# The value projection of the stick-breaking branch: 256 columns for four row tiles, or 512 columns for two row tiles with the weights loaded twice

## The chip, the cores and the metric

The kernel runs on one NeuronCore of a Trainium2 chip. The metric is device time in microseconds (us) of one execution of the whole program. The median of three runs of the kernel before is 725.48 us (725.17 to 725.5). Five engines work beside each other, each through its own queue in order: TensorE (PE; its weight loads are listed apart as PEld), VectorE (DVE), ScalarE (ACT), GpSimd (POOL) and SyncE (SP, which issues nearly all transfers here).

## The reference

One decoder layer on 512 tokens of width 1024, in float32:

```python
h = rms_norm(x, g_mix)
qa, ka, va, qb, kb, vb, gates = split(h @ w_in)      # widths 6 x 512, then 2 x 1024
ya = moba_attention(rope(qa), rope(ka), va)          # 8 heads of 64
yb = stick_breaking_attention(qb, kb, vb)            # 8 heads of 64
g = sigmoid(gates + b_gate)
x = x + (g[0] * (ya @ w_branch_a) + g[1] * (yb @ w_branch_b)) @ w_out
x = x + conv_glu(rms_norm(x, g_ffn))                 # w_up, depthwise conv, silu gate, w_down
out = rms_norm(x, g_final)
```

What the change touches is `vb`, the 512 x 512 values of the stick-breaking branch: `vb = h @ w_in[:, 2560:3072]`, needed by `yb`.

## The kernel before

Float32 products are made from split operands: every weight tile is loaded as 128 x 1024 float32 (512 KB), ACT rounds it to `whi` and DVE takes the rest `wlo = raw - whi` (`wload`, lines 56 to 70). `mm3` (lines 72 to 75) then issues three matmuls per product: hi x hi, hi x lo, lo x hi. A pool of five `raw` tiles and a pool of three split pairs (`wsp`) hold the weights, so a new split may begin once the tile three places ahead of it has been used up.

The attention stage is `attend` (line 390 on), called four times: twice for branch a (MoBA), twice for branch b (stick-breaking), each for two pairs of heads. Each call has nine steps: three `score` steps (matmuls into `sc`, then softmax weights, or for branch b `weights_b`: sigmoids on ACT, a triangular select on POOL, scans of `a` into `R` and products on DVE), six `turn` steps (transposes on PE into `tp`, copied to `aT`), and at the end the product with v into a last `tp` (line 429), split into `ya` or `yb` by ACT (line 435) and DVE (line 436). PE alone is ordered by hand; the other engines' orders are laid down by a scheduler when the program is built.

Between the steps PE runs **fillers**: generators that issue the remaining projections a piece at a time. `fill(gap)` takes the next `gap` units from a list, one unit being three matmuls of 512 columns (or six of 256). `GAPS_A`, `GAPS_A2` and `GAPS_B` hold the gap after each step. The list before is: q and k of the last MoBA heads (32 units), `sb_qk(0)` and `sb_qk(1)` (q and k of a stick-breaking head pair, 16 units each), `vproj_b(0)`, `sb_qk(2)`, `sb_qk(3)`, `vproj_b(1)`, then three gates of 16 units.

All fillers write to two PSUM banks (`pmm`, tiles `mm`). `proj` (one weight tile, 24 matmuls) uses one bank; whoever takes a bank again waits until its last content has been read out. For `sb_qk` that reading is a DVE product into `o` (lines 304 and 306), which is split later by `flush`. `vproj_b(g)` makes columns 256 g to 256 g + 255 of `vb` for all four row tiles: two weight tiles (one for each half of the 1024 inputs), two row tiles side by side in one bank, 24 matmuls of 256 columns for each; a full bank is read out by ACT (line 251) and DVE (line 252), half each.

Of the kernel before, what the change touches and what calls it, by code (L numbers as in the profile page):

```python
# [10 lines left out]
F32 = mybir.dt.float32  # L11
F32R = mybir.dt.float32r
BF = mybir.dt.bfloat16
AF = mybir.ActivationFunctionType
OP = mybir.AluOpType
# [3 lines left out]
S = 512  # L19
D = 1024  # L20
KT = D // 128
QT = S // 128
# [4 lines left out]
NWARM = 9 * (448,) + (128,)  # L27
NP = FT // 2
NL = 3
WORDER = ([(n, k) for n in ("qk0", "va") for k in range(4)] + [("vb", g, h) for g in range(2) for h in range(2)]  # L30
          + [("mqk", n, i) for n in range(2) for i in range(2)] + [("sqk", p, n) for p in range(4) for n in range(2)]
          + [("g", i, b) for i in range(KT) for b in range(2)] + [("ab", i) for i in range(KT)]
          + [("out", k) for k in range(KT)] + [("ox", j) for j in range(KT // 2)] + [("up", i, b) for i in range(FT) for b in range(2)]
          + [("down", k) for k in range(FT)] + [("dx", j) for j in range(NP)])
WIDX = {k: i for i, k in enumerate(WORDER)}
NEG = -1e30
# [3 lines left out]
def trunk_layer(ctx: ExitStack, tc: tile.TileContext, x: bass.AP, xT: bass.AP, w: bass.AP, vec: bass.AP,  # L40
                gfin: bass.AP, trig: bass.AP, out: bass.AP):
    nc = tc.nc

    def pool(stack, name, bufs, space=None, side=None):
        kw = {}
        if space is not None:
            kw["space"] = space
        if side is not None:
            kw["side"] = side
        return stack.enter_context(tc.tile_pool(name=name, bufs=bufs, reuse_waits="tile", **kw))  # L50
# [5 lines left out]
    def wload(key, pieces=1, eng=None):  # L56
        raw = wraw.tile([128, 1024], F32, name="raw")
        hi = wsp.tile([128, 1024], F32R, name="whi")
        lo = wsp.tile([128, 1024], F32R, name="wlo")
        n = 1024 // pieces  # L60
        for i in range(pieces):
            sl = slice(i * n, (i + 1) * n)
            (eng if eng is not None and i == 0 else nc.sync).dma_start(raw[:, sl], w[WIDX[key]][:, sl])
            if eng is not None and i == 0:
                nc.scalar.preload_act_table_set("sqrt_and_others")
        for i in range(pieces):
            sl = slice(i * n, (i + 1) * n)
            nc.scalar.activation(hi[:, sl], raw[:, sl], AF.Copy)  # L68
            nc.vector.tensor_sub(lo[:, sl], raw[:, sl], hi[:, sl].bitcast(F32))  # L69
        return hi, lo  # L70

    def mm3(ps, a, b, start, stop, **kw):
        nc.tensor.matmul(ps, a[0], b[0], start=start, stop=False, **kw)  # L73
        nc.tensor.matmul(ps, a[0], b[1], start=False, stop=False, **kw)  # L74
        nc.tensor.matmul(ps, a[1], b[0], start=False, stop=stop, **kw)  # L75

    def blk(t, k, n=128):
        return t[0][:, k * n:(k + 1) * n], t[1][:, k * n:(k + 1) * n]
# [23 lines left out]
    xg = [hp.tile([128, 2, S], F32R, name=f"xg{k}") for k in range(KT)]  # L102
# [3 lines left out]
    vb = vp.tile([128, QT, 512], F32, name="vb")  # L106

    def rstd_cols(sq, psp, tag, name):
        ps = psp.tile([128, 512], F32, name=tag)
        for t in range(QT):  # L110
            nc.tensor.matmul(ps[:, 2 * t:2 * t + 2], sq[:, t * 128:(t + 1) * 128], ones, start=True, stop=True)
        v = consts.tile([128, QT], F32, name=name + "v")
        nc.vector.tensor_scalar(v, ps[:, 0:2 * QT:2], 1.0 / D, EPS, op0=OP.mult, op1=OP.add)
        return rsqrt(v, QT, name)
# [19 lines left out]
    pmm = pool(psA, "pmm", 2, PSUM)  # L134
# [7 lines left out]
    qk0 = [p1.tile([128, S], F32, name=f"q{j}") for j in range(4)]  # L142
# [18 lines left out]
    for k in range(KT):  # L161
# [7 lines left out]
        else:  # L169
            if k % 2 == 0:  # L170
# [3 lines left out]
                                             op0=OP.mult, op1=OP.subtract)  # L174
# [9 lines left out]
        for n, (i, j) in enumerate(((0, 0), (0, 1), (1, 0))):  # L184
            if k == KT - 1 and n == 2:
                r1 = rstd_cols(ssq, pmm, "mm", "n1")
# [34 lines left out]
    va = mp.tile([128, QT, 512], F32, name="va")  # L221
# [13 lines left out]
        use(ps)  # L235
        yield 1.0

    def vproj_b(g):
        wt = tuple(wload(("vb", g, h)) for h in range(2))
        for t in range(QT):  # L240
            if t % 2 == 0:
                ps = pmm.tile([128, S], F32, name="mm")
            o = ps[:, (t % 2) * 256:(t % 2 + 1) * 256]
            for k in range(KT):
                a = (xg[k][:, 0, t * 128:(t + 1) * 128], xg[k][:, 1, t * 128:(t + 1) * 128])
                mm3(o, a, blk(wt[k // 4], k % 4, 256), k == 0, k == KT - 1)
                if k < KT - 1:
                    yield 0.5
            if t % 2:
                dst = vb[:, t - 1:t + 1, g * 256:(g + 1) * 256]  # L250
                nc.scalar.activation(dst[:, 0], ps[:, :256], AF.Copy, scale=r1[:, t - 1:t])
                nc.vector.tensor_scalar(dst[:, 1], o, r1[:, t:t + 1], None, op0=OP.mult)
            yield 0.5

    def fill(n):
        while n > 0 and fillers:
# [35 lines left out]
    def moba_qk(g):  # L292
        for n in range(2):
            half = {}
            for i in range(2):
                yield from proj(("mqk", n, i), lambda ps: rotate(g, n, i, ps, half))

    def sb_qk(p):
        sc = {}

        def use(n, nm, ps):
            o = hlp.tile([128, S], F32, name="o")
            if nm == "q":
                nc.vector.scalar_tensor_tensor(o, ps, 0.125, rb, op0=OP.mult, op1=OP.mult)
            else:
                nc.vector.tensor_mul(o, ps, rb)
            sc[nm] = mqkp.tile([128, 2, S], F32R, name=f"hl{n}")
            late.append((sc[nm], o))

        for n, nm in enumerate(("q", "k")):  # L310
            yield from proj(("sqk", p, n), lambda ps: use(n, nm, ps))
        stk["b", p] = [(sc["q"], sc["k"], h * 64) for h in range(2)]
# [145 lines left out]
            yield from proj(("g", i, b), lambda ps: use(b, ps))  # L458

    pend = {}  # L460
    fillers = [moba_qk(1), sb_qk(0), sb_qk(1), vproj_b(0), sb_qk(2), sb_qk(3), vproj_b(1)]
    fillers += [gates(i) for i in range(NG)]
    GAPS_A = (12, 0, 5, 5, 0, 5, 7, 5, 5)
    GAPS_A2 = (10, 0, 3, 6, 0, 3, 6, 3, 3)
    GAPS_B = (8, 4, 5, 4, 3, 5, 7, 5, 5)
    attend("a", (0, 1), GAPS_A)
    attend("a", (2, 3), GAPS_A2, True)
    mst.close()
# [1 line left out]
    for p in range(4):  # L470
        yhl["b", p] = ybp.tile([128, 2, S], F32R, name=f"yb{p}")
    gsig = pool(ysta, "gsig", 6, side="right")
    attend("b", (0, 1), GAPS_B)
    attend("b", (2, 3), GAPS_B)
    fill(1000)
    psA.close()
# [3 lines left out]
    pmm = pool(psB, "pmm2", 6, PSUM)  # L480
# [24 lines left out]
    for i in range(KT):  # L505
# [4 lines left out]
        g = pend[i]  # L510
        for b, br in enumerate("ab"):
            ps = pmm.tile([128, S], F32, name="mm")
# [206 lines left out]
    for i in range(FT):  # L719
        uc = []  # L720
        for b in range(2):
            ps = ups.pop(0) if ups else [*up_mm()][-1]
# [3 lines left out]
            t = up.tile([128, S], F32, name=f"t{b}")  # L726
            nc.scalar.activation(t, u, AF.Identity, bias=cb[:, c:c + 1], scale=cw[:, 2, c:c + 1])  # L727
            nc.vector.scalar_tensor_tensor(t[:, 1:], u[:, :S - 1], cw[:, 1, c:c + 1], t[:, 1:],
                                           op0=OP.mult, op1=OP.add)
            nc.vector.scalar_tensor_tensor(t[:, 2:], u[:, :S - 2], cw[:, 0, c:c + 1], t[:, 2:],  # L730
                                           op0=OP.mult, op1=OP.add)
# [12 lines left out]
    dst = ExitStack()  # L744
# [42 lines left out]
    for j in range(NP):  # L787
        xs, wa, w4, _ = ready.pop(0)
# [66 lines left out]
def pack(w_in, w_a, w_b, w_out, w_up, w_down):  # L855
    def rows(m, c):
        return m[:, c].reshape(m.shape[0] // 128, 128, len(c)).transpose(1, 0, 2).reshape(128, -1)

    c128 = np.arange(128)
    t = {}  # L860

    def halves(base, g, i):
        return base + (4 * g + c128 // 32) * 64 + 32 * i + c128 % 32

    first = np.concatenate([halves(base, 0, i) for base in (0, 512) for i in range(2)])
    for k in range(4):
        t["qk0", k] = rows(w_in[k * 256:(k + 1) * 256], first)
    for n, base in enumerate((0, 512)):
        for i in range(2):
            t["mqk", n, i] = rows(w_in, halves(base, 1, i))  # L870
    for j in range(4):
        t["va", j] = rows(w_in[j * 256:(j + 1) * 256], 1024 + np.arange(512))
    for g in range(2):
        for h in range(2):
            t["vb", g, h] = rows(w_in[h * 512:(h + 1) * 512], 2560 + g * 256 + np.arange(256))
    for p in range(4):
        for n, base in enumerate((1536, 2048)):
            t["sqk", p, n] = rows(w_in, base + p * 128 + c128)
    for i in range(KT):
        for b in range(2):  # L880
            t["g", i, b] = rows(w_in, 3072 + b * 1024 + i * 128 + c128)
        t["ab", i] = np.concatenate([rows(w_a, i * 128 + c128), rows(w_b, i * 128 + c128)], axis=1)
        t["out", i] = w_out[i * 128:(i + 1) * 128]
    for j in range(KT // 2):
        t["ox", j] = np.concatenate([w_out[(2 * j + b) * 128:(2 * j + b + 1) * 128, 512:] for b in range(2)], axis=1)
    for i in range(FT):
        for b in range(2):
            t["up", i, b] = rows(w_up, b * FF + i * 128 + c128)
        t["down", i] = w_down[i * 128:(i + 1) * 128]
    for j in range(NP):  # L890
        t["dx", j] = np.concatenate([w_down[(2 * j + b) * 128:(2 * j + b + 1) * 128, 512:] for b in range(2)], axis=1)
    return np.ascontiguousarray(np.stack([t[k] for k in WORDER]))

# [27 lines left out]
```

## Time and profile before

| | us |
|---|---|
| median of three runs | 725.48 |
| the profiled execution | 725.86 |
| its span, first to last instruction | 724.0 |
| PE busy in the span | 714.3 |
| DVE busy | 554.1 |
| ACT busy | 346.6 |

The profiled execution lies 0.38 us above the median; the trace begins at 0 us with its first instruction. A timeline row gives the start, the busy time, the engine, the line, the operation, its output and inputs, shapes and count, and in brackets the idle time before it and what ended that. Consecutive instructions of one line and operation are merged into one row with a count, even where their shapes differ. A matmul's duration is longer than the distance to the next one's start, since matmuls are pipelined; what a matmul costs is that distance.

### The profile page before, as it was taken

How to read it: one execution, taken by the hardware profiler on the slowest of the kernel's cores; microseconds unless marked ns; L12 is line 12 of the kernel's file. 1: busy time of each engine (PE TensorE's matmuls, PEld its weight loads, DVE VectorE, ACT ScalarE, POOL GpSimd, SP SyncE). 2: the span in 40 equal slices, each digit the busy share in tenths (PEclk: the TensorE clock that was granted, in tenths of full speed). 3: DMA queues.
4: the chain of work that ended last, by engine and by line, in shares of the span. 5: the costliest groups of instructions: out<-in, count | busy, mean ns of one | idle time of the engine just before them, and what ended most of it. 6: DMA issues, size and time to landing. Idle time of an engine off the chain costs nothing.

```text
span 724.0 us, 9741 instructions
## 1 busy us (share of the span) xinstructions
PE 714.3 (99%) x3792; PEld 593.1 (82%) x3792; DVE 554.1 (77%) x795; ACT 346.6 (48%) x506; POOL 22.7 (3%) x40
## 2 busy tenths in 40 slices
PE   9999999999999999999999999999999999999995
PEld 6888888889888888888888888888888888788884
DVE  7778867593973654669878787787787789878996
ACT  6435535463663232337484434443434444556665
POOL 0000000230410000000000000000000000000000
PEclk9999999999999999999999999999999999999998
DMA  8522111021132223225744223223223223467703
GB/s 306 193 88 88 60 59 59 31 88 59 60 96 74 94 87 107 82 103 191 279 148 139 87 88 116 87 88 115 89 88 112 92 88 113 139 213 238 262 24 118
DMA packets 25679, 84.11 MB, mean 116 GB/s; under 512 B 2848, under 2 KB 3488, under 8 KB 25632
## 3 DMA queue, kind: packets, MB, share of 16 engines
q1 hardware_dynamic: 24912, 82.30, 33.8%
q10 hardware_dynamic: 720, 1.18, 0.4%
q8 instruction: 30, 0.49, 0.3%
q14 instruction: 17, 0.14, 0.1%
HBM read 79.27 MB, written 4.19 MB: 115 GB/s over the span
## 4 chain that ended last, share of the span: by engine, by line
PE 95%; DVE 3%; ACT 1%; issue 1%; ACTq 0%
PE b L74 13%; PE b L75 13%; PE b L73 12%; PE mm L73 11%; PE mm L75 11%; PE mm L74 11%; PE c L74 4%; PE c L75 4%; PE c L73 4%; PE q L188 3%; PE tp L429 2%; PE tp L407 2%; PE sc L330 1%; PE sc L340 1%; PE mm L145 1%
## 5 line engine op out<-in xcount | busy, mean ns | idle before, releaser
L68 ACT ACTIVATE whi<-raw 128x1024 fp32r<-128x1024 f32 (+2 forms) x98 | 98.2, 1008 | 166.7 <-PE b L74 80.7
L74 PE MATMUL b<-h,whi 128*128 128x512 f32 x352 | 137.1, 389 | 0.3 <-DVE h L634 0.3
L73 PE MATMUL b<-h,whi 128*128 128x512 f32 x352 | 137.1, 390 | 0.0
L75 PE MATMUL b<-h,wlo 128*128 128x512 f32 x352 | 137.0, 389 | 0.0
L69 DVE TENSOR_TENSOR wlo<-raw,whi 128x1024 fp32r<-128x1024 f32 (+2 forms) x98 | 112.9, 1157 | 14.6 <-ACT whi L68 14.3
L73 PE MATMUL mm<-xg,whi 128*128 128x512 f32 x224 | 90.0, 402 | 0.0
L75 PE MATMUL mm<-xg,wlo 128*128 128x512 f32 x224 | 87.5, 390 | 0.0
L74 PE MATMUL mm<-xg,whi 128*128 128x512 f32 x224 | 87.3, 390 | 0.0
L74 PEld LDWEIGHTS b<-h,whi 128*128 128x128 f32 x352 | 66.1, 188 | 14.3 <-DVE h L634 0.7
L73 PEld LDWEIGHTS b<-h,whi 128*128 128x128 f32 x352 | 66.1, 188 | 13.8
L75 PEld LDWEIGHTS b<-h,wlo 128*128 128x128 f32 x352 | 66.1, 188 | 13.6
L556 ACT ACTIVATE whi<-raw 128x1024 fp32r<-128x1024 f32 x45 | 46.7, 1051 | 33.3 <-DVE raw L568 20.2
L556 DVE TENSOR_TENSOR wlo<-raw,whi 128x1024 fp32r<-128x1024 f32 x45 | 54.3, 1219 | 4.4 <-ACT whi L556 4.4
L725 DVE TENSOR_TENSOR u<-b,rb 128x512 f32<-128x512 f32 x44 | 30.3, 690 | 30.4 <-PE b L75 30.3
L73 PEld LDWEIGHTS mm<-xg,whi 128*128 128x128 f32 x224 | 42.1, 188 | 10.1 <-issue 1.8
L75 PEld LDWEIGHTS mm<-xg,wlo 128*128 128x128 f32 x224 | 42.0, 188 | 9.1
L74 PEld LDWEIGHTS mm<-xg,whi 128*128 128x128 f32 x224 | 42.2, 188 | 7.9
L727 ACT ACTIVATE t<-u,vecs 128x512 f32<-128x512 f32 x44 | 35.2, 802 | 2.1 <-DVE u L725 2.1
L74 PE MATMUL c<-wlo,xa 128*128 128x512 f32 x88 | 34.4, 391 | 0.4 <-DVE wlo L556 0.4
L73 PE MATMUL c<-whi,xa 128*128 128x512 f32 x88 | 34.3, 389 | 0.0
L75 PE MATMUL c<-whi,xa 128*128 128x512 f32 x88 | 34.2, 389 | 0.0
L730 DVE SCALAR_TENSOR_TENSOR t<-u,vecs,t 128x510 f32<-128x510 f32 x44 | 32.9, 749 | 1.3
(219 smaller groups left out, 1260.3 us busy)
## 6 DMA issues: line engine op xcount, KB each, us to landing
raw<-w SPq DMA_DIRECT2D x133, 512.0 KB, 3.3
xk<-xT SPq DMA_DIRECT2D x8, 256.5 KB, 5.6
x<-x SPq DMA_DIRECT2D x4, 512.0 KB, 6.8
x1D<-x SPq DMA_DIRECT2D x8, 256.0 KB, 3.2
x1R<-x1D SPq DMA_DIRECT2D x4, 512.0 KB, 8.1
raw<-w SPq DMA_DIRECT2D x6, 256.0 KB, 5.8
out<-on SPq DMA_DIRECT2D x4, 256.0 KB, 2.2
out<-on ACTq DMA_DIRECT2D x4, 256.0 KB, 2.4
```

What stands on the lines that cost most here:

```text
L68: nc.scalar.activation(hi[:, sl], raw[:, sl], AF.Copy)
L69: nc.vector.tensor_sub(lo[:, sl], raw[:, sl], hi[:, sl].bitcast(F32))
L73: nc.tensor.matmul(ps, a[0], b[0], start=start, stop=False, **kw)
L74: nc.tensor.matmul(ps, a[0], b[1], start=False, stop=False, **kw)
L75: nc.tensor.matmul(ps, a[1], b[0], start=False, stop=stop, **kw)
L188: nc.tensor.matmul(qk0[c], w0[i][:, (k % 2) * 512 + c * 128:(k % 2) * 512 + (c + 1) * 128], xg[k][:, j], start=(k == 0 and n == 0), stop=( ...
L407: nc.tensor.transpose(tp[:, h, c:c + 128], a[:, h, c:c + 128], ident)
L429: nc.tensor.matmul(av[h * 64:(h + 1) * 64, j, qt * 128:(qt + 1) * 128], v[:, kb, (2 * p + h) * 64:(2 * p + h + 1) * 64], aT[p][:, h, o + k ...
L556: splits.append((nc.scalar.activation(hi, raw, AF.Copy), nc.vector.tensor_sub(lo, raw, hi.bitcast(F32))))
L725: nc.vector.tensor_mul(u, ps, rb2)
L727: nc.scalar.activation(t, u, AF.Identity, bias=cb[:, c:c + 1], scale=cw[:, 2, c:c + 1])
L730: nc.vector.scalar_tensor_tensor(t[:, 2:], u[:, :S - 2], cw[:, 0, c:c + 1], t[:, 2:], op0=OP.mult, op1=OP.add)
```

## The change

`vproj_b(T)` now makes all 512 columns of `vb` for row tiles 2T and 2T + 1. It holds both banks, one for each row tile, and goes through four weight tiles of 256 inputs x 512 columns each, which are laid out as those of `va` are. `vproj_b(0)` and `vproj_b(1)` each load all four, so eight weight tiles are loaded and split where there were four. The first row tile's bank is read out by ACT, the second's by DVE, 512 columns in one instruction. In the list of fillers both calls stand ahead of `sb_qk(2)` and `sb_qk(3)`. The first branch-b call of `attend` takes its gaps from a new tuple `GAPS_B1` with 52 units in place of 46. The number of units over all fillers is unchanged, 176; the four calls' gaps sum to 170 before and 176 after.

```diff
-WORDER = ([(n, k) for n in ("qk0", "va") for k in range(4)] + [("vb", g, h) for g in range(2) for h in range(2)]
+WORDER = ([(n, k) for n in ("qk0", "va", "vb") for k in range(4)]
...
-    def vproj_b(g):
-        wt = tuple(wload(("vb", g, h)) for h in range(2))
-        for t in range(QT):
-            if t % 2 == 0:
-                ps = pmm.tile([128, S], F32, name="mm")
-            o = ps[:, (t % 2) * 256:(t % 2 + 1) * 256]
-            for k in range(KT):
-                a = (xg[k][:, 0, t * 128:(t + 1) * 128], xg[k][:, 1, t * 128:(t + 1) * 128])
-                mm3(o, a, blk(wt[k // 4], k % 4, 256), k == 0, k == KT - 1)
-                if k < KT - 1:
-                    yield 0.5
-            if t % 2:
-                dst = vb[:, t - 1:t + 1, g * 256:(g + 1) * 256]
-                nc.scalar.activation(dst[:, 0], ps[:, :256], AF.Copy, scale=r1[:, t - 1:t])
-                nc.vector.tensor_scalar(dst[:, 1], o, r1[:, t:t + 1], None, op0=OP.mult)
-            yield 0.5
+    def vproj_b(T):
+        ps = [pmm.tile([128, S], F32, name="mm") for _ in range(2)]
+        for j in range(4):
+            wt = wload(("vb", j))
+            for i in range(2):
+                t = 2 * T + i
+                for k in range(2 * j, 2 * j + 2):
+                    a = (xg[k][:, 0, t * 128:(t + 1) * 128], xg[k][:, 1, t * 128:(t + 1) * 128])
+                    mm3(ps[i], a, blk(wt, k % 2, 512), k == 0, k == KT - 1)
+                    if k < KT - 1:
+                        yield 1.0
+                if j == 3:
+                    if i:
+                        nc.vector.tensor_scalar(vb[:, t], ps[i], r1[:, t:t + 1], None, op0=OP.mult)
+                    else:
+                        nc.scalar.activation(vb[:, t], ps[i], AF.Copy, scale=r1[:, t:t + 1])
+                    yield 1.0
...
-    fillers = [moba_qk(1), sb_qk(0), sb_qk(1), vproj_b(0), sb_qk(2), sb_qk(3), vproj_b(1)]
+    fillers = [moba_qk(1), sb_qk(0), sb_qk(1), vproj_b(0), vproj_b(1), sb_qk(2), sb_qk(3)]
...
+    GAPS_B1 = (8, 4, 6, 5, 3, 6, 8, 6, 6)
...
-    attend("b", (0, 1), GAPS_B)
+    attend("b", (0, 1), GAPS_B1)
```

The first place is PE at the start of `vproj_b(0)`, around the transposes of one `turn` step, the last six of which fall here (`tp`; `mm` is the bank, numbers tell buffers apart). Before:

```order
L73 MATMUL mm_1333<-whi_1322,xg3_95 128x256
L74 MATMUL mm_1333<-wlo_1323,xg3_95 128x256
L75 MATMUL mm_1333<-whi_1322,xg3_95 128x256
L407 MATMUL tp_1346<-ident_67,a1_1197 128x128 [waits DVE_49,Activation_49]
L407 MATMUL tp_1346<-ident_67,a1_1197 128x128 x2
L407 MATMUL tp_1346<-ident_67,a1_1197 128x128 [waits DVE_49]
L407 MATMUL tp_1346<-ident_67,a1_1197 128x128 x2
L73 MATMUL mm_1333<-whi_1328,xg4_96 128x256
```

Now:

```order
L73 MATMUL mm_1321<-whi_1324,xg1_93 128x512
L74 MATMUL mm_1321<-wlo_1325,xg1_93 128x512
L75 MATMUL mm_1321<-whi_1324,xg1_93 128x512
L408 MATMUL tp_1335<-ident_67,a1_1197 128x128 [waits DVE_49,Activation_49]
L408 MATMUL tp_1335<-ident_67,a1_1197 128x128 x2
L408 MATMUL tp_1335<-ident_67,a1_1197 128x128 [waits DVE_49]
L408 MATMUL tp_1335<-ident_67,a1_1197 128x128 x2
L73 MATMUL mm_1322<-whi_1324,xg0_92 128x512 [waits DVE_49]
```

After the transposes PE went on in the same bank; now it takes the second bank, which held k of `sb_qk(1)`, and waits for DVE, whose reading of that bank is `o` on line 306.

The second place is PE where `vproj_b(0)` ends and `vproj_b(1)` begins, behind the first branch-b scores. Now:

```order
L74 MATMUL mm_1322<-wlo_1409,xg7_99 128x512
L75 MATMUL mm_1322<-whi_1408,xg7_99 128x512
L73 MATMUL mm_1554<-whi_1557,xg0_92 128x512 [waits Activation_49]
L74 MATMUL mm_1554<-wlo_1558,xg0_92 128x512
L75 MATMUL mm_1554<-whi_1557,xg0_92 128x512
L73 MATMUL mm_1554<-whi_1557,xg1_93 128x512
L74 MATMUL mm_1554<-wlo_1558,xg1_93 128x512
L75 MATMUL mm_1554<-whi_1557,xg1_93 128x512
L73 MATMUL mm_1555<-whi_1557,xg0_92 128x512 [waits DVE_49]
```

`mm_1555` is the bank of `mm_1322`, six matmuls after `mm_1322` was finished. Before, the bank taken next at this place was the one that ACT and DVE had read out eight units earlier.

The third place is DVE at the same point of the program; its reading of `mm_1322` is the row with `vb`. Before:

```order
L378 SCALAR_TENSOR_TENSOR R_1548<-a1_1536 128x128 [waits Pool_49]
L436 TENSOR_TENSOR ya3_88<-tp_1451,ya3_88 128x512 [waits Activation_49]
L378 SCALAR_TENSOR_TENSOR R_1548<-a1_1536 128x128
L378 SCALAR_TENSOR_TENSOR R_1548<-a1_1536 128x256 [waits Pool_49]
L378 SCALAR_TENSOR_TENSOR R_1548<-a1_1536 128x256
L380 TENSOR_TENSOR a2_1538<-a2_1538,R_1548 128x2x128 [waits DVE_49,Pool_49]
L380 TENSOR_TENSOR a2_1538<-a2_1538,R_1548 128x2x256 [waits DVE_49,Pool_49]
```

Now:

```order
L379 SCALAR_TENSOR_TENSOR R_1517<-a1_1505 128x128 [waits Pool_49]
L437 TENSOR_TENSOR ya3_88<-tp_1420,ya3_88 128x512 [waits Activation_49]
L379 SCALAR_TENSOR_TENSOR R_1517<-a1_1505 128x128
L379 SCALAR_TENSOR_TENSOR R_1517<-a1_1505 128x256 [waits Pool_49]
L379 SCALAR_TENSOR_TENSOR R_1517<-a1_1505 128x256
L381 TENSOR_TENSOR a2_1507<-a2_1507,R_1517 128x2x128 [waits DVE_49,Pool_49]
L251 TENSOR_SCALAR vb_104<-mm_1322,n1r_339 128x512 [waits PE_49]
L381 TENSOR_TENSOR a2_1507<-a2_1507,R_1517 128x2x256 [waits DVE_49,Pool_49]
```

The scans (named SCALAR_TENSOR_TENSOR here, TENSOR_TENSOR_SCAN in the trace) of the first pair of heads and the first product stand ahead of the reading of `mm_1322`; the second product now stands behind it.

## Rows read from the trace of the kernel before

**Rows 1.** The page: busy time of PE, and the chain that ended last.

```profile
PE 714.3 (99%) x3792; PEld 593.1 (82%) x3792; DVE 554.1 (77%) x795; ACT 346.6 (48%) x506; POOL 22.7 (3%) x40
...
PE 95%; DVE 3%; ACT 1%; issue 1%; ACTq 0%
```

**Rows 2.** Timeline of PE, 117 to 124 us: start, busy us, instruction, count.

```profile
117.55 0.28 PE L73 MATMUL mm<-whi,xg 128*128 128x256 f32 x1
...
118.96 0.82 PE L407 MATMUL tp<-ident,a 128*128 128x128 f32 x6
119.54 0.36 PE L73 MATMUL mm<-whi,xg 128*128 128x256 f32 x1
119.74 0.28 PE L74 MATMUL mm<-wlo,xg 128*128 128x256 f32 x1
...
123.80 0.28 PE L75 MATMUL mm<-whi,xg 128*128 128x256 f32 x1
```

**Rows 3.** Timeline of PE, 134 to 144 us: first branch-b scores and what follows.

```profile
134.57 1.64 PE L340 MATMUL sc<-hl,hl 64*128 64x128 f32 x24
136.14 0.39 PE L73 MATMUL mm<-whi,xg 128*128 128x256 f32 x1
...
138.15 0.39 PE L75 MATMUL mm<-xg,wlo 128*128 128x512 f32 x1
...
141.56 0.39 PE L75 MATMUL mm<-xg,wlo 128*128 128x512 f32 x1
...
143.14 0.50 PE L73 MATMUL mm<-xg,whi 128*128 128x512 f32 x1
```

**Rows 4.** Timeline of DVE at 119 us: k of `sb_qk(1)` read out.

```profile
119.12 0.68 DVE L306 TENSOR_TENSOR o<-mm,rb 128x512 f32<-128x512 f32 x1
```

**Rows 5.** Timeline of DVE, 137 to 146 us: scans and products of branch b.

```profile
137.91 0.60 DVE L378 TENSOR_TENSOR_SCAN R<-a 128x128 f32<-128x128 f32 x1 [1.91 <-POOL a L370]
...
140.84 0.55 DVE L380 TENSOR_TENSOR a<-a,R 128x256 f32<-128x256 f32 x1
...
141.32 0.88 DVE L380 TENSOR_TENSOR a<-a,R 128x512 f32<-128x512 f32 x1
...
142.12 2.10 DVE L378 TENSOR_TENSOR_SCAN R<-a 128x128 f32<-128x128 f32 x4
...
144.87 1.21 DVE L69 TENSOR_TENSOR wlo<-raw,whi 128x1024 fp32r<-128x1024 f32 x1
```

**Rows 6.** Groups by form, 49 to 178 us: busy us, mean ns of one, idle before.

```profile
L69 DVE TENSOR_TENSOR wlo<-raw,whi 128x1024 fp32r<-128x1024 f32 x15 | 18.5, 1230 | 3.7 <-ACT whi L68 3.7
...
L68 ACT ACTIVATE whi<-raw 128x1024 fp32r<-128x1024 f32 x15 | 16.0, 1067 | 11.4 <-PE mm L75 5.6 <-PE mm L74 2.8 <-issue 2.1
...
L264 DVE TENSOR_TENSOR hl<-o,hl 128x512 fp32r<-128x512 f32 x8 | 5.9, 737 | 1.0 <-ACT hl L263 1.0
...
L263 ACT ACTIVATE hl<-o 128x512 fp32r<-128x512 f32 x8 | 5.1, 636 | 2.1 <-DVE o L304 1.1 <-DVE o L306 0.8
...
L215 DVE TENSOR_SCALAR va<-mm,n1r 128x512 f32<-128x512 f32 x1 | 0.8, 751 | 0.6 <-PE mm L75 0.6
```

**Rows 7.** Stretches: us, then PE, PEld, DVE, ACT, POOL busy, PEclk, DMA share, GB/s.

```profile
117.00:131.00 14.00, 14.00 (x127) 13.73 (x128) 9.47 (x14) 6.22 (x13) 0.00 (x0) 1.00 0.12 39
131.00:150.00 19.00, 19.00 (x166) 16.11 (x163) 13.96 (x23) 11.57 (x16) 7.44 (x11) 1.00 0.17 56
```

**Rows 8.** DMA issues of the page: count, KB each, median us to landing.

```profile
raw<-w SPq DMA_DIRECT2D x133, 512.0 KB, 3.3
```

**Rows 9.** Timelines: product with v of the third and behind the fourth `attend` call.

```profile
176.21 4.59 PE L429 MATMUL tp<-aT,vb 128*64 128x128 f32 x80
...
226.35 0.50 PE L73 MATMUL mm<-xg,whi 128*128 128x512 f32 x1
...
228.45 0.69 DVE L436 TENSOR_TENSOR yb<-tp,yb 128x512 fp32r<-128x512 f32 x1 [0.66 <-ACT yb L435]
```

**Rows 10.** The end of the span in stretches (columns as in Rows 7).

```profile
716.00:717.00 1.00, 0.32 (x2) 0.00 (x0) 1.00 (x4) 0.83 (x3) 0.00 (x0) 1.00 0.49 195
...
719.00:720.00 1.00, 0.00 (x0) 0.00 (x0) 0.93 (x3) 0.59 (x1) 0.00 (x0) 0.74 0.94 358
```

**Rows 11.** Timeline of PE at the start of the program.

```profile
1.30 3.65 PE L145 MATMUL mm<-warmb 128*128 128x448 bf16 x10 [1.30 <-DVE R L375]
4.90 2.66 PE L188 MATMUL q<-xg,whi 128*128 128x512 f32 x8
...
8.31 1.98 PE L188 MATMUL q<-xg,whi 128*128 128x512 f32 x8
```

More of the change, by code (lines that the diff above doesn't have):

```diff
@@ L871, in pack @@
     for j in range(4):
[L872 to L875, printed above, removed]
+        for n, base in (("va", 1024), ("vb", 2560)):
+            t[n, j] = rows(w_in[j * 256:(j + 1) * 256], base + np.arange(512))
     for p in range(4):
```

## The prediction

> **What bounds the kernel now.** I read the page first: PE is busy 99% of the span and holds 95% of the chain that ended last [rows 1]. So the question is not which engine is loaded, but whether PE ever stands still around the change. The timeline of PE answers it: between 117.55 and 124 us, and again between 136.14 and 143.14 us, each matmul starts one matmul's distance after the last, and no row names a releaser [rows 2, 3]. What makes PE shorter or later here therefore reaches the end of the program one for one, unless a later wait swallows it; and no wait is there to swallow it. The timeline of DVE at the same places tells when a bank is read out [rows 4, 5], and the stretches tell how much room DVE, ACT and the DMA engines have [rows 7]. The profiled execution took 725.86 us, 0.38 above the median of 725.48; the sum is made against the former, and the 0.38 is taken off at the end. A measurement of this kernel can tell about 0.2%, 1.45 us, from no change: under 724.03 is faster, over 726.93 slower.
>
> **Wider matmuls.** `vb` took 192 matmuls of 256 columns and now takes 96 of 512. Matmuls overlap, so the price is the distance between starts. From 119.74 to 123.80 us there are 34 distances: 4.06 / 34 = 0.1194 us for 256 columns [rows 2]. From 138.15 to 141.56 us there are 15: 3.41 / 15 = 0.2273 us for 512 [rows 3]. That is 192 x 0.1194 - 96 x 0.2273 = 22.92 - 21.82 = **-1.10 us**. With 0.120 for the narrow and 0.227 for the wide ones it is -1.25, with 0.119 and 0.2275 it is -1.0; the steps that interrupt the fillers are as many as before. [...]
>
> **The first new wait.** `vproj_b(0)` needs its second bank six matmuls and one step of transposes after its first. That bank held k of `sb_qk(1)`, which DVE reads on line 306. PE starts the filler at 117.55 us; six wide matmuls bring it to 118.91, the six transposes take 0.58 more (118.96 to 119.54 [rows 2]): 119.49. DVE's reading runs from 119.12 for 0.68 us [rows 4] and ends at 119.80, and some 0.05 pass until PE sees it. So PE waits **+0.36 us** (0.3 to 0.4). Before, the bank was not needed for another 36 narrow matmuls.
>
> **The second new wait** is the main one, where `vproj_b(1)` takes the bank of `mm_1322`, six matmuls after `vproj_b(0)` has filled it. I count from the start of the branch-b scores at 134.57 us, so that a shift of PE ahead of it cancels: what DVE does here is released by these scores and by the product with v just ahead of them. The scores end at 136.14 [rows 3]; twelve wide matmuls follow, six that fill `mm_1322` and six into the other bank, the first with some 0.1 us extra as behind the scores: PE arrives at 136.14 + 0.11 + 12 x 0.227 = 138.97. DVE could read the bank at 137.6, but in its queue the reading stands behind both parts of `ya3`, four scans and the first product. In the trace the first scan waits 1.91 us for POOL until 137.91, and the first product starts at 140.84; the second, whose place the reading takes, starts at 141.32 [rows 5]. A read-out of 128x512 from a bank by DVE took 0.751 us [rows 6], so it ends at 142.07, and PE goes on at 142.12: **+3.15 us**. The bounds: nothing at all if DVE read the bank as soon as it was full (138.4, before PE arrives), and 3.45 if the scans run 0.3 later. I take 3.15 because DVE works in order and each row of that chain is in the trace. Behind the waiting matmul stand 12 of `vproj_b(1)` and the next scores; behind the read-out stand the second product and the four scans of the other pair, 0.8 us later than before.
>
> **What costs nothing, and why.** Four more weight tiles mean four splits of 1.230 us on DVE (4.9 us) and 1.067 on ACT (4.3 us) [rows 6], and four more loads of 512 KB in SP's queue. DVE is idle for 4.5 of 14 us in 117 to 131 us and for 5.0 of 19 in 131 to 150, ACT for over 7 in each, and the DMA engines are busy 12 to 17% [rows 7]; a load lands 3.3 us after its issue [rows 8] and is issued up to five tiles ahead, each tile 12 x 0.227 = 2.7 us of PE. The nearest to being late is the third tile of `vproj_b(1)`: its `wlo` stands behind the second product and the second four scans. Those start 0.8 later than before, so at 142.07 + 0.80, take 2.03, and `wlo` takes 1.21 [rows 5]: ready at 146.1. PE needs it after the rest of its two tiles and the second scores, 142.12 + 12 x 0.227 + 1.35 + 6 x 0.23 = 147.6 (1.35 is 143.14 - 141.56 less one matmul [rows 3]): 1.5 us to spare, which goes first if the scans slip further. The read-outs are four of 512 columns for eight of 256, on the same engines. k of `sb_qk(3)` is now finished two units ahead of the product with v of its call: product 0.68, split 0.64 on ACT and 0.74 on DVE, behind at most one weight split of 1.23, is 3.3 us [rows 4, 6], against 6 x 0.227 + 4.59 = 5.9 us of PE [rows 9]. Behind the last product with v the fillers are used up, where before 18 matmuls of a gate (4.1 us) were left: DVE's last split of `yb` ends at 228.45 + 0.69 = 229.14, and PE needs it 12 matmuls after 226.35, at 226.35 + 0.33 + 11 x 0.227 = 229.18 [rows 9]. That is a tie, 0 to 0.3 us; I take 0.
>
> **The sum**: -1.10 + 0.36 + 3.15 = +2.41, so 728.27 for the profiled execution and, less 0.38, **727.9 us** against the median, 0.33% slower. Its own range is 727.2 to 728.6: -0.15 from the width, 0.3 either way from the scans, 0.3 from the tail.
>
> **Rivals.**
> *A, not slower.* The mechanism is DVE reaching the read-out sooner: the place is the scans on DVE behind POOL. If PE's second wait is 2.2 us or less, the whole is within 0.2%; under 0.74 us it is no slower at all, and with none the sum is -0.74: 724.7. For it speaks that the scans hang on a chain over ACT and POOL with 1.91 us of idleness on DVE in it [rows 5], whose length may change as other work moves. Against it: that chain starts with the scores, as PE's count does, and the order of DVE is fixed. 0.22.
>
> *B, PE's clock falls.* The wait is a stretch of over 3 us without matmuls, at a granted clock that the page shows as 1.00. [...] I give it 0.11.
>
> *C, the weights are late too.* If the scans that stand ahead of the third tile's `wlo` slip by more than the 1.5 us worked out above (DVE takes another split ahead of them, say), PE waits a third time, by 1 to 1.5 us: 729.2. 0.09.
>
> The forecast keeps 0.58.
>
> **How the numbers follow.** Forecast, B and C are slower by over 0.2%: 0.78. Of A's 0.22, I put 0.16 to a second wait of 0.05 to 2.2 us (724.7 to 726.9; within 0.2%) and 0.06 to the case that both waits vanish and the wide matmuls come at 0.223 us or less (22.92 - 96 x 0.223 = 1.5), under 724.03. The range of 726.0 to 730.6 takes in the forecast, B, C and the upper half of A, and leaves out about 0.12 below and 0.06 above.
>
> **What would show it.** In the changed profile: 96 fewer matmuls (3,696), all of `vb`'s of 128x512; a first matmul into `mm` on line 73 with an idle time of about 3.2 us released by DVE's `vb` (now line 251), starting some 7.5 us after the first branch-b scores begin, and one of about 0.4 us released by `o` (now line 307); 102 weight splits of `wload` for 98 and 137 loads of 512 KB for 133; a chain with a few more us of DVE in it; and a granted clock that stays 1.00 across the wait. If the wait by DVE is there and the time isn't, the price of the matmuls is wrong; if the wait isn't there, DVE read the bank early and A holds; if the clock shows less than 1.00 behind 142 us, B does. A PE wait on `wlo` near 146 us is C, one on `hl` near 181 us or on `yb` near 229 us shows a slack that I took for enough and wasn't.

## The result

The changed kernel takes 730.79 us (median of four runs, 729.70 to 731.43) against 725.49: a ratio of 1.007 (95% interval 1.0059 to 1.0082). It is slower, as forecast, but by 5.3 us where 2.4 was the forecast: well above the forecast's own 727.2 to 728.6, and 0.2 us above 730.6, the upper end of the range that takes in the rivals. A second set of five runs beside other kernels gave 730.38, 1.0064 (1.0052 to 1.0077), inside that range. Both waits of the forecast are there, in their places and of their sizes; the rival B, the fall of PE's clock, came on top.

The page after, busy times and loads:

```profile
PE 714.7 (98%) x3696; PEld 588.3 (81%) x3696; DVE 557.8 (77%) x797; ACT 350.5 (48%) x508; POOL 21.4 (3%) x40
...
L69 DVE TENSOR_TENSOR wlo<-raw,whi 128x1024 fp32r<-128x1024 f32 (+2 forms) x102 | 117.6, 1159 | 13.1 <-ACT whi L68 12.9
...
raw<-w SPq DMA_DIRECT2D x137, 512.0 KB, 3.3
```

96 matmuls fewer than before [rows 1], four splits and four loads more. The timeline of PE after (the rows at the two new waits, and what follows the second):

```profile
118.20 0.82 PE L408 MATMUL tp<-ident,a 128*128 128x128 f32 x6
119.14 0.50 PE L73 MATMUL mm<-whi,xg 128*128 128x512 f32 x1
...
133.83 1.65 PE L341 MATMUL sc<-hl,hl 64*128 64x128 f32 x24
...
138.07 0.39 PE L75 MATMUL mm<-whi,xg 128*128 128x512 f32 x1
141.37 0.80 PE L73 MATMUL mm<-whi,xg 128*128 128x512 f32 x1 [2.91 <-DVE vb L251]
141.96 0.63 PE L74 MATMUL mm<-wlo,xg 128*128 128x512 f32 x1
142.39 0.63 PE L75 MATMUL mm<-whi,xg 128*128 128x512 f32 x1
...
144.09 0.56 PE L73 MATMUL mm<-whi,xg 128*128 128x512 f32 x1
144.49 0.40 PE L74 MATMUL mm<-wlo,xg 128*128 128x512 f32 x1
```

The first matmul into the second bank starts 0.94 us after the transposes began; these take 0.58 [rows 2], so PE waits 0.36. The second wait ends 141.37 - 133.83 = 7.54 us behind the start of the scores; the forecast had 142.12 - 134.57 = 7.55. DVE after, where [rows 5] showed the two products back to back:

```profile
140.10 0.55 DVE L381 TENSOR_TENSOR a<-a,R 128x256 f32<-128x256 f32 x1
140.58 0.74 DVE L251 TENSOR_SCALAR vb<-mm,n1r 128x512 f32<-128x512 f32 x1
141.24 0.67 DVE L381 TENSOR_TENSOR a<-a,R 128x512 f32<-128x512 f32 x1
```

Then comes what the forecast's sum did not hold: the next matmuls start 0.43 us apart instead of 0.227. The stretches after (columns as in rows 7, PEclk third from the end):

```profile
131.00:140.00 9.00, 7.46 (x90) 6.27 (x86) 3.52 (x6) 6.02 (x8) 2.84 (x6) 1.00 0.18 58
140.00:142.00 2.00, 0.63 (x2) 0.54 (x3) 2.00 (x5) 0.20 (x1) 1.28 (x3) 0.76 0.00 0
142.00:143.00 1.00, 1.00 (x4) 0.81 (x3) 1.00 (x3) 0.00 (x0) 0.00 (x0) 0.50 0.00 0
143.00:144.00 1.00, 1.00 (x4) 0.81 (x3) 1.00 (x3) 0.00 (x0) 0.00 (x0) 0.50 0.00 0
144.00:145.00 1.00, 1.00 (x5) 0.75 (x5) 1.00 (x3) 0.62 (x1) 0.00 (x0) 0.78 0.00 0
145.00:146.00 1.00, 1.00 (x6) 0.60 (x6) 1.00 (x3) 0.45 (x1) 0.00 (x0) 1.00 0.06 8
```

The granted clock fell to 0.50 at 141.03 us, while PE stood idle, and was back at 1.00 from 144.44. From 141.37 to 144.49 seven matmuls took 3.12 us where 7 x 0.227 makes 1.59: 1.5 us.

**One measure for all runs.** An execution's total holds differences that have nothing to do with the change: the profiled one of after had its first scores at 50.16 us, the one of before at 50.87, with the same program up to there. So I compare the stretch from the first mask matmul of branch a to the first product with `yb`, which holds all that was changed. Timeline of PE before:

```profile
50.87 0.62 PE L322 MATMUL sc<-maskb,identb 128*128 128x128 bf16 x8
...
233.28 0.39 PE L73 MATMUL mm<-yb,whi 128*128 128x512 f32 x1
```

and after, with the last matmul ahead of `yb`:

```profile
50.16 0.62 PE L323 MATMUL sc<-maskb,identb 128*128 128x128 bf16 x8
...
236.51 0.39 PE L75 MATMUL mm<-ya,wlo 128*128 128x512 f32 x1
236.82 0.47 PE L73 MATMUL mm<-yb,whi 128*128 128x512 f32 x1
```

182.41 before, 186.66 after: +4.25. In the table each kernel's stretch is against 182.41, and its median against that of the kernel before in the same set.

| kernel | stretch | median | ratio (95%) |
|---|---|---|---|
| changed | +4.25 | 730.79 against 725.49 | 1.007 (1.0059 to 1.0082) |
| changed, again | +4.42 | 730.38 against 725.42 | 1.0064 (1.0052 to 1.0077) |
| complete ahead of the scores | +0.79 | 726.97 against 725.6 | 1.0018 (1.0009 to 1.0027) |
| busy while waiting | +2.83 | 729.27 against 725.6 | 1.0049 (1.0037 to 1.0062) |
| both read-outs exchanged | +5.47 | 731.47 against 725.6 | 1.0083 (1.007 to 1.0097) |
| exchanged in the first alone | +1.35 | 727.25 against 725.42 | 1.0025 (1.0016 to 1.0034) |
| before, four tiles more | +2.54 | 728.64 against 725.6 | 1.0044 (1.0031 to 1.0056) |
| before, new order | +0.24 | 725.5 against 725.42 | 0.9996 (0.9987 to 1.0005) |
| one more split pair | +7.15 | 733.02 against 725.42 | 1.0098 (1.0084 to 1.0112) |
| the same, placed later | -0.46 | 724.91 against 725.65 | 0.9987 (0.9978 to 0.9996) |
| the same, one unit moved | +0.98 | 727.13 against 725.65 | 1.0021 (1.0012 to 1.003) |

The medians lie up to 1.05 us further up than the stretch says, or 0.3 lower. The profiled execution of before was 0.38 above its own median, and that of the changed kernel, 729.70, is the fastest of its four, 1.09 below theirs. Behind the stretch, where the program is the same, the trace of the changed kernel is 0.47 us longer (491.16 against 490.68 to the end of the span). So of the 5.3 us between the medians about 1 is not explained by the change's own stretch, and stays open.

### The profile page after: what moved, and what is told of

It reads as the page before. It is cut to its first block, busy times and chain, and to the rows that moved or that the text cites. A ratio compares the mean times of both kernels' runs of the same rounds, so it can differ in the third digit from the quotient of the medians.

```text
span 728.0 us, 9567 instructions
## 1 busy us (share of the span) xinstructions
PE 714.7 (98%) x3696; PEld 588.3 (81%) x3696; DVE 557.8 (77%) x797; ACT 350.5 (48%) x508; POOL 21.4 (3%) x40
## 4 chain that ended last, share of the span: by engine, by line
PE 82%; issue 9%; DVE 5%; ACT 2%; POOL 1%; ACTq 0%; POOLq 0%; DVEq 0%
PE b L74 12%; PE b L75 12%; PE b L73 12%; PE mm L73 8%; PE mm L74 8%; PE mm L75 8%; PE c L74 4%; PE c L75 4%; PE c L73 4%; PE q L188 3%; PE tp L408 1%; PE tp L430 1%; PE sc L331 1%; POOL a L371 1%; DVE R L379 1%
## 5 line engine op out<-in xcount | busy, mean ns | idle before, releaser
L68 ACT ACTIVATE whi<-raw 128x1024 fp32r<-128x1024 f32 (+2 forms) x102 | 102.5, 1009 | 167.5 <-PE b L74 80.4
L69 DVE TENSOR_TENSOR wlo<-raw,whi 128x1024 fp32r<-128x1024 f32 (+2 forms) x102 | 117.6, 1159 | 13.1 <-ACT whi L68 12.9
L735 ACT ACTIVATE t<-t 128x512 f32<-128x512 f32 x22 | 13.9, 631 | 42.0 <-DVE t L732 42.0
```

What stands on the lines that cost most here:

```text
L735: nc.scalar.activation(uc[0], uc[0], AF.Silu)
```

## The experiments

**Complete ahead of the scores.** Two units move ahead of the last product with v of branch a.

```diff
-    GAPS_A2 = (10, 0, 3, 6, 0, 3, 6, 3, 3)
-    GAPS_B1 = (8, 4, 6, 5, 3, 6, 8, 6, 6)
+    GAPS_A2 = (10, 0, 3, 6, 0, 3, 6, 3, 5)
+    GAPS_B1 = (6, 4, 6, 5, 3, 6, 8, 6, 6)
```

> Two of the eight units behind the first branch-b scores are moved ahead of the last product with v of branch a, so that vproj_b(0) is complete 6 us before those scores. Nothing is left out. Theory (the second wait, 3.15 us, and the halved clock behind it, 1.5 us in the trace of the changed kernel): both go, leaving -1.1 for the width, +0.36 for the first wait and +0.2 in the tail: 724.9 to 725.9, no idle time of PE over 0.5 us between 118 and 232 us, granted clock 1.00 there. Rival (weights loaded twice are what costs): the load is the same, so 728 or more.

726.97: the second wait and the fall of the clock are gone (1.00 in all of 117 to 153 us), 3.8 us of the loss at one stroke, but it is 1.1 us above the upper end of what was expected. PE waits at a new place, the first tile of `sb_qk(2)`:

```profile
151.76 0.40 PE L74 MATMUL mm<-xg,whi 128*128 128x512 f32 x1
153.09 0.50 PE L75 MATMUL mm<-xg,wlo 128*128 128x512 f32 x1 [0.94 <-DVE wlo L69]
```

The split that it waits for stands on DVE behind scans that leave it no gap:

```profile
148.26 0.95 DVE L379 TENSOR_TENSOR_SCAN R<-a 128x384 f32<-128x384 f32 x1
...
149.13 2.79 DVE L379 TENSOR_TENSOR_SCAN R<-a 128x384 f32<-128x384 f32 x3
151.84 1.19 DVE L69 TENSOR_TENSOR wlo<-raw,whi 128x1024 fp32r<-128x1024 f32 x1
```

So the rival of the double load is not void either: while PE waited 3 us, DVE caught up, and without the wait the extra splits show.

**Busy while waiting.** Twelve matmuls without use where PE waits.

```diff
+                if T and i and not j:
+                    junk = ptr.tile([128, 2, 512], F32, name="tp")
+                    for n in range(12):
+                        nc.tensor.matmul(junk[:, 0], xg[0][:, 0, :128], wt[0][:, :512], start=True, stop=True)
```

> The changed kernel with 12 matmuls of 512 columns more (2.7 us, their result is thrown away) just where PE waits for the second bank of vproj_b(1), into the bank of the transposes. The wait for DVE stays: PE goes on at the same 7.5 us behind the start of the scores, but is busy until 0.5 us before. Theory (the clock falls because PE stands idle): granted clock 1.00 throughout, the matmuls behind the wait 0.227 us apart, and the time falls by what the clock cost, 1.5 to 2.6 us: 728.2 to 729.3. Rival (the clock falls for another reason, or the slow matmuls cost nothing): 730.5 or more.

729.27. The timeline of PE in this run, and its stretches:

```profile
139.22 2.98 PE L247 MATMUL tp<-whi,xg 128*128 128x512 f32 x12
142.09 0.50 PE L73 MATMUL mm<-whi,xg 128*128 128x512 f32 x1
142.43 0.39 PE L74 MATMUL mm<-wlo,xg 128*128 128x512 f32 x1
```

```profile
140.00:142.00 2.00, 2.00 (x10) 1.50 (x8) 2.00 (x5) 0.92 (x1) 2.00 (x4) 1.00 0.00 0
142.00:143.00 1.00, 1.00 (x5) 0.78 (x5) 1.00 (x4) 0.00 (x0) 0.00 (x0) 1.00 0.00 0
```

With the scores at 134.55, PE goes on at 7.54 us behind them, just as in the changed kernel; only the clock differs, and the kernel is faster than the changed one: by 1.3 to 1.6 us in the medians, each against the kernel before of its set, by 1.4 to 1.6 in the stretch. With PE busy the clock stays at 1.00 in 142 to 143 us, where the changed kernel has 0.50: here it fell because PE stood idle, and that is what it cost.

**The read-outs exchanged.**

```diff
-                    if i:
+                    if not i:
                         nc.vector.tensor_scalar(vb[:, t], ps[i], r1[:, t:t + 1], None, op0=OP.mult)
```

> The changed kernel with the two read-outs exchanged: DVE takes the first row tile's bank, ACT the second's. On ACT the reading stands behind both sigmoids of both pairs, which in the trace end some 5.3 us behind the start of the scores; a read-out of 0.7 lets PE go on at 6.0, and PE arrives at 4.4: a wait of 1.6 us instead of 3.15. Theory (the clock falls only behind the long wait): clock 1.00, 730.8 - 1.55 - 1.5 to 2.6 = 726.6 to 727.8. Rival (any wait costs the clock): 729 or more.

731.47, far from the 726.6 to 727.8 expected, and in the stretch 1.1 to 1.2 us more than the changed kernel. The wait behind the scores is as expected, ending 140.69 - 134.62 = 6.07 us behind their start, and a second one comes that I had not looked for:

```profile
140.69 0.50 PE L73 MATMUL mm<-whi,xg 128*128 128x512 f32 x1 [1.43 <-ACT vb L253]
...
155.59 0.50 PE L73 MATMUL mm<-xg,whi 128*128 128x512 f32 x1 [2.27 <-DVE vb L251]
```

At the end of `vproj_b(1)` it is now DVE that must free the bank which q of `sb_qk(2)` takes, behind two weight splits. The stretches of this run:

```profile
140.00:142.00 2.00, 1.31 (x6) 1.09 (x7) 2.00 (x4) 1.58 (x3) 2.00 (x4) 1.00 0.00 0
...
155.00:156.00 1.00, 0.41 (x2) 0.37 (x3) 1.00 (x2) 0.73 (x2) 0.41 (x1) 1.00 0.70 197
156.00:157.00 1.00, 1.00 (x5) 0.81 (x4) 1.00 (x2) 0.00 (x0) 0.00 (x0) 0.79 0.77 270
157.00:158.00 1.00, 1.00 (x4) 0.71 (x4) 0.59 (x2) 0.00 (x0) 0.00 (x0) 0.50 0.75 246
```

After 1.43 us of idleness the clock stayed at 1.00; after 2.27 it fell to 0.50, and only when PE had been at work again for some time (from 155.59; the mean of 0.79 in 156 to 157 puts the fall near 156.6).

**Exchanged in `vproj_b(0)` alone** (`if i == T:` on the same line).

> The changed kernel with the read-outs exchanged in vproj_b(0) alone. The wait behind the first scores is 1.6 us as in the run with both exchanged, without a fall of the clock; the banks of vproj_b(1) are read as in the changed kernel, so the wait of 2.4 us and the halved clock behind it go. Theory (the two waits are independent, DVE's order makes each): 730.8 - 1.55 - 1.54 = 727.7, up to 728.3 if the weight tile of sb_qk(2) is then waited for by up to 0.6 us. Rival (the exchange itself costs): 729 or more.

727.25, a little better than expected; 3.1 us less than the changed kernel in the same set. One wait of 1.43 us for ACT is left, the second is gone, and the clock is 1.00 from 138 to 144 us:

```profile
140.15 0.50 PE L73 MATMUL mm<-whi,xg 128*128 128x512 f32 x1 [1.43 <-ACT vb L253]
```

**Four tiles more in the kernel before**, used by nothing.

```diff
         wt = wload(key)
+        if key[0] == "sqk" and key[1] > 1:
+            wload(key)
```

> The kernel before with four weight tiles of 512 KB more, loaded and split by ACT and DVE, one behind each tile of sb_qk(2) and sb_qk(3), and used by nothing. PE's work is as before. Theory (the double loading is hidden): 725.5, within 0.4 us either way. Rival (DVE, ACT or the DMA engines have no room for four tiles): 726.5 or more, with PE waiting for wlo or whi.

728.64: here my theory fell. PE never waits for a weight; it waits for ACT, twice for its copies of the transposes and, for 0.47 us at 155.35, once with scores for its `a`. The two copies:

```profile
150.36 0.88 PE L409 MATMUL tp<-ident,a 128*128 128x128 f32 x6 [0.56 <-ACT aT L412]
...
163.52 0.88 PE L409 MATMUL tp<-ident,a 128*128 128x128 f32 x6 [0.85 <-ACT aT L412]
```

In ACT's order a rounding stands ahead of these copies, and before it ACT stands for 4.80 us until DVE has split another tile:

```profile
145.50 1.06 ACT L68 ACTIVATE whi<-raw 128x1024 fp32r<-128x1024 f32 x1 [4.80 <-DVE wlo L69]
```

Idle time in a stretch (5.0 of 19 us on DVE [rows 7]) did not make room for a split here: DVE's order and the three pairs of buffers decided whether it fits. In the changed kernel the four tiles fall elsewhere (two of them ahead of the scores), so the 2.5 us need not be its price; this run does not show what that is.

**The new order alone**, with 256 columns.

```diff
-    fillers = [moba_qk(1), sb_qk(0), sb_qk(1), vproj_b(0), sb_qk(2), sb_qk(3), vproj_b(1)]
+    fillers = [moba_qk(1), sb_qk(0), sb_qk(1), vproj_b(0), vproj_b(1), sb_qk(2), sb_qk(3)]
...
+    GAPS_B1 = (8, 4, 6, 5, 3, 6, 8, 6, 6)
```

> The kernel before (256 columns, each weight tile loaded once) with nothing but the new order of the fillers and the new gaps. Theory (order and gaps cost only the tail, where DVE's split of yb is waited for: 0.34 us in the trace of the changed kernel): 725.6 to 726.2, no wait for a bank near the branch-b scores. Rival (the order itself makes waits): 726.6 or more.

725.5, 0.9996 (0.9987 to 1.0005): nothing that can be measured; +0.24 in the stretch, of which the tail is only 0.09 (worked out below, with the tail). The loss comes from the two-bank `vproj_b`, not from the order.

**One more pair of split buffers**, with the units moved as in the first experiment.

```diff
+        hi = (to or wsp).tile([128, 1024], F32R, name="whi")
+        lo = (to or wsp).tile([128, 1024], F32R, name="wlo")
...
+            wt = wload(("vb", j), to=wxp if T and j == 1 else None)
...
+    GAPS_B = (8, 4, 5, 4, 3, 5, 7, 5, 4)
```

> The run with vproj_b(0) complete ahead of the scores, with one more pair of buffers for split weights, used by the second tile of vproj_b(1) alone, so that DVE splits one tile more while it waits for the last product with v of branch a; and the last gap of branch b one unit shorter, so that three matmuls of a gate stand ahead of the first product with yb. Theory (what that run lost was the 1.1 us of PE's wait for wlo of sb_qk(2), since DVE has no idle time between the scores and there, and 0.34 us in the tail): both go, leaving -1.1 + 0.36 = -0.74: 724.4 to 725.5. Rival (DVE is late elsewhere then): 726.3 or more.

733.02, a miss. The free buffers let the scheduler put the rounding of that tile early in ACT's order, ahead of its transfer:

```profile
109.60 1.06 ACT L68 ACTIVATE whi<-raw 128x1024 fp32r<-128x1024 f32 x1 [4.62 <-DMA raw<-w]
```

The softmax behind it came late, PE waited 4.60 us, until 114.57, for DVE's copy `aT`, and the clock fell again (0.77 in 112 to 114 us, 0.50 in 114 to 118).

**The same, placed later**: for the last tile, held behind DVE's last copy of branch a, and with more of the gate left for the tail.

```diff
+                if T and j == 3:
+                    after.enter_context(tc.issue_after(copied[-1]))
+                wt = wload(("vb", j), to=wxp if T and j == 3 else None)
...
+    GAPS_B = (8, 4, 5, 4, 3, 5, 7, 4, 3)
```

> As the run with one more pair of split buffers, but used by the last tile of vproj_b(1), its split held back behind DVE's last copy of branch a (there ACT waited 4.6 us for a transfer in the middle of branch a); and the last two gaps of branch b shorter by one and two units, so that nine matmuls of a gate stand ahead of the first product with yb. Theory (weights twice cost DVE time at one place only; the rest is the width): the waits of 4.8 us at 110 us, of 1.1 us for wlo of sb_qk(2) and of 0.34 us for yb go, the one of 0.36 us at the start of vproj_b(0) stays: -1.1 + 0.36 = -0.74, so 724.3 to 725.4 with the kernel before at 725.45. Rival (DVE is late at yet another place): 726.2 or more.

724.91, as expected, 0.9987 (0.9978 to 0.9996): 0.13% below the kernel before, with an interval that just leaves out 1, and less than the 0.2% that the forecast takes for distinguishable. The stretch gives -0.46 where -0.74 was expected, so that the median agrees so well is partly luck. The kernel before did not get the further buffers and gaps, so this does not show that the wide matmuls alone gain. The place where PE waited in the first experiment, and the first product with `yb`:

```profile
151.61 0.48 PE L73 MATMUL mm<-xg,whi 128*128 128x512 f32 x1
151.93 0.40 PE L74 MATMUL mm<-xg,whi 128*128 128x512 f32 x1
152.16 0.40 PE L75 MATMUL mm<-xg,wlo 128*128 128x512 f32 x1
...
233.17 0.39 PE L73 MATMUL mm<-yb,whi 128*128 128x512 f32 x1
```

**One unit moved** ahead of the last MoBA scores as well.

```diff
-    GAPS_A2 = (10, 0, 3, 6, 0, 3, 6, 3, 5)
+    GAPS_A2 = (10, 0, 3, 7, 0, 2, 6, 3, 5)
```

> The same with one unit moved ahead of the last MoBA scores, so that k of sb_qk(1) is complete before them and DVE reads it ahead of the row maxima. Theory (the first wait came from the 2.4 us of maxima ahead of that reading): the wait of 0.36 us goes too, leaving -1.1: 723.9 to 725.0, and PE has no idle time over 0.3 us between 60 and 240 us. Rival (the steps of branch a, now 0.7 us later or nearer to each other, wait instead): 725.3 or more.

727.13, the rival's case. The first wait is gone (the matmul behind the transposes of 119.07 starts at 119.65), but ACT now stands 3.39 us ahead of a rounding until its transfer lands, and the transposes at 125.18 wait for it:

```profile
125.18 1.10 PE L412 MATMUL tp<-ident,a 128*128 128x128 f32 x8 [1.19 <-ACT aT L415]
```

**The changed kernel again.**

> The changed kernel once more, unaltered, beside the others on the same chip. Theory: 730.3 to 731.3; the profile shows the wait of 3.1 us at 7.5 us behind the first branch-b scores and the granted clock at 0.5 behind it for 2.5 to 5 us, the matmuls there 0.427 apart; the more matmuls at half clock, the longer the execution. Rival (the fall of the clock was chance): clock 1.00 and 729.3 or less.

730.38, with the wait of 2.91 us at 142.16 and the fall behind it:

```profile
142.00:143.00 1.00, 0.84 (x3) 0.73 (x4) 1.00 (x4) 0.00 (x0) 0.07 (x1) 0.84 0.00 0
...
145.00:146.00 1.00, 1.00 (x4) 0.82 (x3) 1.00 (x4) 0.81 (x1) 0.00 (x0) 0.50 0.00 0
```

Here the clock fell near 142.7, half a microsecond after PE had gone on, so more of the fall lay on matmuls than in the first trace: eight were slow where there it was seven, and the stretch is 0.17 us longer.

## Why the forecast was right, and where it was too small

**The first wait** (+0.36 forecast): 0.36. Right, and from its cause: with one unit moved, where DVE reads k ahead of the row maxima, it is gone.

**The second wait** (+3.15): by the count of the forecast, PE would have arrived 4.40 us behind the start of the scores; it went on at 7.54. Right, and its cause is DVE's order: with ACT as the reader it ends at 6.07, with the bank full earlier there is none.

**The tail** (0, "a tie, 0 to 0.3"): 236.51 to 236.82 is 0.08 more than a matmul. The new order alone shows +0.24 in the stretch, and its tail is 0.09 of it; the rest is a wait that neither the forecast nor an expectation had, ahead of six transposes of the fourth `attend` call. Before, and after:

```profile
207.46 0.39 PE L75 MATMUL mm<-xg,wlo 128*128 128x512 f32 x1
207.69 0.82 PE L407 MATMUL tp<-ident,a 128*128 128x128 f32 x6
```

```profile
214.69 0.39 PE L75 MATMUL mm<-xg,wlo 128*128 128x512 f32 x1
215.16 0.88 PE L408 MATMUL tp<-ident,a 128*128 128x128 f32 x6
```

The transposes start 0.47 us behind the last matmul instead of 0.23, right behind the end of ACT's previous copy `aT` (215.11), and the next matmul comes 0.63 behind them instead of 0.57: 0.30 in all. The runs with the new order have it, the placed-later one too. The kernel before has a pause of 0.14 at 144.66 instead, which these runs have lost. So order and tail together are 0.30 + 0.09 - 0.14 = 0.25.

**The width** (-1.10): four runs give it, each by its stretch less its other terms. Placed later, without the tail: -0.46 - 0.36 - 0.30 + 0.14 = -0.98. Busy while waiting: 2.83 - 0.36 - 3.14 - 0.25 = -0.92. Exchanged in the first alone: 1.35 - 0.36 - 1.67 (6.07 - 4.40) - 0.25 = -0.93. Complete ahead: 0.79 - 0.36 - 1.1 - 0.25 = -0.92. So about -0.95, 0.1 to 0.2 less than forecast. The distances were nearly right: over the whole stretch, behind the first matmul after a step, they are in the trace of before on average 0.229 us at 512 columns and 0.119 at 256; where the rest goes is open.

**The clock** (rival B, left out of the sum, 0.11): +1.5. This is the step that failed. What I took as a sign that 3 us of idleness are just bearable was the end of the program before: the last matmul ends at 716.32 us, and the clock is 1.00 up to 719 and on average 0.74 in 719 to 720 [rows 10]. The stretches between:

```profile
717.00:718.00 1.00, 0.00 (x0) 0.00 (x0) 0.93 (x5) 0.75 (x3) 0.00 (x0) 1.00 0.74 283
718.00:719.00 1.00, 0.00 (x0) 0.00 (x0) 0.47 (x4) 0.73 (x2) 0.00 (x0) 1.00 0.63 242
```

One such fall is no measure: it comes 3.2 us behind the end of the last matmul (719.48), the one at the end of the changed kernel's trace 4.9 us behind (724.71 against 719.83), and the one at the second wait 2.6 us behind (141.03 against 138.46). The runs show idle times of 2.27, 2.91 (twice) and 4.60 us with a fall and two of 1.43 without.

The price was wrong too. I had put it at 2.6 us, which makes B's 730.5 and the upper end of the range; no run shows a fall of 2.6, and the trace of the changed kernel shows 1.5. The 2.6 was my estimate from the program's start [rows 11], where the profile shows a clock of 1.00:

```profile
2.00:4.00 2.00, 2.00 (x7) 0.84 (x6) 0.00 (x0) 0.52 (x1) 0.00 (x0) 1.00 0.85 282
```

The trace of before has no record of the clock ahead of 6.10 us, and the profile counts what is not recorded as 1.00. The pace there is that of the matmuls at 0.50: the warm matmuls start 0.373 us apart, which is 1.20 columns a ns (448 / 373), and the second and third of 512 columns behind them 0.43 (5.49 and 5.92), as behind the second wait. So the row was a price of the clock, but of some 4.8 us of work at that pace (1.30 to 6.10), where the second wait has 3.1 behind it (141.37 to 144.44). What a fall cost is in the matmul's own distance: 0.43 for 0.227, 0.2 us for each of the seven to nine matmuls until it rose again, behind the waits of 2.27 and 2.91 us. That B's 730.5 lies so near the measured median is therefore luck: 1.1 us too much for the clock stand against the 1 us of the medians that no trace explains.

**What costs nothing** (four more tiles): true in the changed kernel's trace, where PE waits for no weight, but for a reason that I had not given. It is the second wait that gives DVE the time; where that wait is taken away, 1.1 us of the load shows, at the first tile of `sb_qk(2)` (rival C had put such a wait at the third tile of `vproj_b(1)`).

The sum with measured terms: -0.95 + 0.36 + 3.14 + 1.5 + 0.25 = 4.30, against 4.25 and 4.42 in the two traces of the changed kernel. In the medians the change costs 5.0 to 5.3.

One sign that I named did not serve: the chain of waits after is

```profile
PE 82%; issue 9%; DVE 5%; ACT 2%; POOL 1%; ACTq 0%; POOLq 0%; DVEq 0%
```

and the run that has lost both the wait and the fall (placed later) has the same shares, so the 5% of DVE do not measure the wait.

## What to carry over

When a projection takes both banks at once, whoever takes a bank next comes early: write down for each bank who frees it, and what stands ahead of that reading on its engine. A long wait of PE in this kernel is to be priced with the half-clock matmuls behind it: every wait of 2.27 us and more in these runs had them, and behind the one of 2.91 they cost 1.5 us, half as much again. Cover that a stall provides is gone when the stall is repaired, so look next at what the stall was hiding.

## What I had not expected of the hardware

The clock fell after PE was at work again: with both read-outs exchanged the idle time ended at 155.59 us, the clock was 1.00 up to 156 and 0.50 in 157 to 158, so the matmuls that paid were not those next to the wait; the second trace of the changed kernel shows the same, 0.5 us behind its wait (0.84 in 142 to 143, 0.50 in 143 to 144). And the wait of 1.43 us cost its length only (clock 1.00 in 140 to 142, distances of 0.23 behind the first matmul), while the one of 2.27 us cost some 1.5 us more: the matmuls behind it start 0.43 us apart from 156.68 to 159.66.
